# A two-layer attention and retention trunk on one core: value products a round later, the first span outputs in column parts, later sines, evenly pulled side work, rows turned and outputs stored in one

## The chip, the cores and the metric

The kernel runs on one core of a Trainium2 chip. A core has a matrix engine (TensorE; PE in the profile, PEld for its weight loads), a vector engine (DVE), a scalar engine (ACT), GpSimd (POOL), and SyncE (SP), which issues the DMA transfers here. The metric is the time of one execution on the device in microseconds (us). The kernel before takes 2097.04 us, the median of three runs (2094.75 to 2097.13).

## What is computed

Two layers over a sequence of 2048 tokens of width 1024 (float32), then a last RMS norm. In each layer half of the mixing width goes through chunked softmax attention (8 heads of 64; a token sees its chunk of 64 and the 8 chunks before, with a relative bias), the other half through retention (4 heads of 128, rotary phases, decays per head):

```python
def hybrid_layer(x, norm_gain, w_in, w_out, rel_bias, cos, sin):
    hn = rms_norm(x, norm_gain)
    aq, ak, av, ag, rq, rk, rv, rg = jnp.split(hn @ w_in, cuts, axis=-1)
    ya = chunked_rel_attention(aq, ak, av, rel_bias)
    yr = chunkwise_retention(rq, rk, rv, cos, sin)
    y = jnp.concatenate([ya * jax.nn.silu(ag), yr * jax.nn.silu(rg)], axis=-1)
    return x + y @ w_out
```

## The kernel before

**Precision.** Products run in float16 with three terms: every operand is split into a high half and a low remainder, and high times high, high times low and low times high are summed.

**Tiles.** Tokens go in 16 tiles of 128, four of which make a span (n = 0 to 3, 512 columns). The heads go in four groups s: two attention heads and one retention head each. For each layer l, group s and span n there are two stages. `dense_T` (L608) makes four outputs with the tokens in columns, j = 0 to 3: queries, keys, retention queries, retention keys; each is 24 matmuls of 512 columns (three terms, eight slices of the width) in three rounds of eight, into one of two accumulators (psD). `dense_V` (L738) makes values and gates for the span's four token tiles, a = 0 to 3, again 24 matmuls in three rounds each. After it, ACT and DVE empty the accumulator (L760 to L770); the tanh of the gates (L761) lies in a buffer `gt` (five of them), which later holds the gate.

**Rounds.** `run()` (L1152) sets the order of everything. In each round it emits eight dense matmuls, then what `later(k, fn)` (L595) had deferred to this round, then one step of the attention of the span before, then some steps of side work, taken by `pull` from generators that were handed to `push` (L1128). It pulls the whole number above (open steps)/(rounds left).

**Attention.** `attention` (L778) takes eight units (four tiles, two heads), three rounds each: in the first `qk`, in the second a part of the decayed retention product, in the third the retention product. `qk` (L785) makes the scores S on PE (L800, L801; one PSUM buffer); DVE adds the bias and takes the maximum (L804), turns it into the exponent's offset (L806); ACT takes the exponential (L807) and copies it to a high half (L809), POOL subtracts for the low half (L810), and a round later SP transposes both halves by DMA (L812) into `pT` (two buffers). The scores lie in buffers of tag `sc`, the halves in `pq`, two of each. The value product `pv` (L815 to L822) of a unit runs six rounds after its scores, at the start of the round of the unit after next, ahead of that unit's scores. A round later `out_` divides by the sum of weights, multiplies by the gate (L826 to L832), and for the second head stores both heads' columns to y in DRAM (L835).

**Retention.** `decayed` (L870) makes the product of keys and queries and writes it masked to the next 128 columns of its PSUM tile; `retention` (L884) adds the carried state, and `fin` (L923) applies norm and gate and stores to y.

**Normalized rows.** `norms_from_input` (L1166), `residual` (L987) and, for y, the output stage make rows of 1024 in a high and a low half: `rows_hi` (L225, ACT), `rows_lo` (L229, DVE), then `transpose_rows` (L235): two DMA transposes on SP (L236, L237) into `hTh` and `hTl`. The rows lie in the attention's `sc` and `pq` buffers (`row_pair`, L221).

**Rotary tables.** `tables` (L83) works out cosines and sines of one span in small steps of side work; the two sines are L121 and L122, and eight stores follow (L129 to L132). `dense_T` loads the tables of a span in two DMAs (L616, L617).

**Output stage.** `wout` (L1066) multiplies y's tiles with the output weights, six rounds per tile (L1105), while the last span's attention still runs. Per tile it loads y, squares it on ACT into its row buffer (`y_squares`, L955), scales, makes the halves and turns them (`y_turn`, L966); `wout_first` (L1053) does this for the first two tiles as side work, in ten steps.

**Order on the queues.** The order on PE, ACT, DVE and POOL is the order of emission, by hand. The order on SP follows a planner's cost model, except at the start, where it is written out. An instruction that waits holds up all behind it on its engine.

Of the kernel before, what the change touches and what calls it, by code (L numbers as in the profile page):

```python
# [18 lines left out]
P = 128  # L19
# [8 lines left out]
def hybrid_trunk(ctx: ExitStack, tc: tile.TileContext, x, pos, gain, gcol, w_in, w_out, rel, fgain,  # L28
# [33 lines left out]
    pool.memset(mhalf, -0.5)  # L62
    invf_sb = cp.tile([P, 1], F32, tag="invf", name="invf_sb")
# [6 lines left out]
    tab_d = [dp.tile([2, P, 512], F32, tag=f"tab{n}", name=f"tab{n}") for n in range(NS)]  # L70
# [12 lines left out]
    def tables(n, wk):  # L83

        ang, k, r, k2 = wk
# [34 lines left out]
        yield  # L120
        act.activation(r, ang, AF.Sin)  # L121
# [4 lines left out]
        for hf in range(2):  # L126
            sl = slice(hf * 64, hf * 64 + 64)
            cs = slice(hf * 256, hf * 256 + 256)
            sp.dma_start(tab_d[n][0, 0:64, cs], k2[sl, :])  # L129
            sp.dma_start(tab_d[n][0, 64:128, cs], k2[sl, :])  # L130
            sp.dma_start(tab_d[n][1, 0:64, cs], ang[sl, :])
            sp.dma_start(tab_d[n][1, 64:128, cs], r[sl, :])  # L132
# [3 lines left out]
    TAB_STEPS = 19  # L136
# [78 lines left out]
    def hT_of(l, n):  # L215
        if (l, n) not in hT:
            hT[l, n] = (hp.tile([P, KT, 512], F16, tag="hTh", name=f"hTh{l}_{n}"),
                        hp.tile([P, KT, 512], F16, tag="hTl", name=f"hTl{l}_{n}"))
        return hT[l, n]

    def row_pair(nm):  # L221
        return (b2.tile([P, 1280], F16, tag="sc", name=f"rh{nm}")[:, 0:D],
                b2.tile([P, 1280], F16, tag="pq", name=f"rl{nm}")[:, 0:D])
# [11 lines left out]
    def transpose_rows(rows, dh, dl):  # L235
        sp.dma_start_transpose(out=dh, in_=rows[0])  # L236
        sp.dma_start_transpose(out=dl, in_=rows[1])  # L237

    class Tok:


        def __init__(self, t, xt, rows):
            self.t, self.x, self.rows, self.nm = t, xt, rows, f"n0_{t}"
            self.hh, self.hl = (h_[:, :, t % 4 * P:(t % 4 + 1) * P] for h_ in hT_of(0, t // 4))
# [21 lines left out]
        def hi(self):  # L266
            if self.rows:
                self.rw = (self.rows[:, 0:D], self.rows[:, D:2 * D])
                act.activation(self.rw[0], self.x, AF.Copy)
                return  # L270
# [3 lines left out]
        def lo(self):  # L274
            if self.rows:
                dve.tensor_tensor(self.rw[1], self.x, self.rw[0], op=ALU.subtract)
                return
# [4 lines left out]
        def dma(self):  # L282
            transpose_rows(self.rw, self.hh, self.hl)
# [324 lines left out]
    def dense_T(l, s, n, g, st):  # L608
        hh, hl = hT[l, n]
        nm = f"{l}_{s}_{n}"  # L610
        st.tabc = b1.tile([P, 512], F32, tag="tabc", name=f"tabc{nm}")
        st.tabs = b1.tile([P, 512], F32, tag="tabs", name=f"tabs{nm}")
# [14 lines left out]
        def evacuate(j, ps):  # L627
            if j == 0:
                st.q = b2.tile([P, 2, 2, 512], F16, tag="q", name=f"q{nm}")
                qq = b1.tile([P, 2, 512], F16, tag="qq", name=f"qq{nm}")  # L630
# [10 lines left out]
            elif j == 1:  # L641
                st.k = b3.tile([P, 2, 512], F16, tag="k", name=f"k{nm}")
                kk = b1.tile([P, 2, 512], F16, tag="swp", name=f"kk{nm}")
                kh, kl = kk[:, 0, :], kk[:, 1, :]
                act.activation(kh, ps, AF.Copy, scale=2.0 ** -16)

                def k_rest():
                    dve.scalar_tensor_tensor(out=kl, in0=ps, scalar=2.0 ** -16, in1=kh, op0=ALU.mult, op1=ALU.subtract)
                    sp.dma_start(st.k[0:64, 0, :], kh[0:64, :])
                    sp.dma_start(st.k[64:128, 1, :], kh[64:128, :])  # L650
                    sp.dma_start(st.k[64:128, 0, :], kl[0:64, :])
                    sp.dma_start(st.k[0:64, 1, :], kl[64:128, :])

                soon(k_rest)
            else:
                w = 5 - j
                rot = b2.tile([P, w, 512], F16, tag=f"rot{j}", name=f"rot{nm}_{j}")
                if j == 2:
                    raw = rot[:, 1:3].rearrange("p a c -> p (a c)").bitcast(F32)
                else:  # L660
                    raw = b1.tile([P, 512], F32, tag="qq", name=f"raw{nm}")
                act.activation(raw, ps, AF.Copy, scale=2.0 ** -16)

                def swap(rot=rot, raw=raw, j=j):
                    swp = b1.tile([P, 512], F32, tag="swp", name=f"swp{nm}_{j}")
# [20 lines left out]
                    later(d, turned(raw, raw, st.tabc, ALU.mult))  # L686
                    later(d + 1, turned(swp, swp, st.tabs, ALU.mult))
# [30 lines left out]
        for j in range(2 if first else 0, 4):  # L718
# [19 lines left out]
    def dense_V(l, s, n, g, st):  # L738
        hh, hl = hT[l, n]
# [38 lines left out]
    def attention(l, s, n, g, st, prev, nxt):  # L778
# [4 lines left out]
        ya = {}  # L783

        def qk(a, hx):  # L785
# [10 lines left out]
            for j0, j1 in zip(cuts, cuts[1:]):  # L796
# [5 lines left out]
            v = b2.tile([P, 640], F32, tag="sc", name=f"sc{u.nm}")[:, 0:w]  # L802
            m = b2.tile([P, 1], F32, tag="mq", name=f"mq{u.nm}")
            dve.tensor_tensor_reduce(out=v, in0=S[:, 0:w], in1=g.bias[hx][:, 640 - w:640], scale=1.0, scalar=-3.0e38,  # L804
                                     op0=ALU.add, op1=ALU.max, accum_out=m)
            dve.tensor_scalar(m, m, g.nc[:, 0:1], LN_PSC, op0=ALU.mult, op1=ALU.add)  # L806
            act.activation(v, v, AF.Exp, bias=m[:, 0:1], scale=g.c[:, 0:1])  # L807
            pq = b2.tile([P, 1280], F16, tag="pq", name=f"pq{u.nm}")
# [6 lines left out]
        def pv(u):  # L815
            t = 4 * n + u.a
            o = psR.tile([P, 512], F32, tag="small", name=f"o{u.nm}")
            for b, (q_, a_) in enumerate(u.kts):
# [3 lines left out]
                pe.matmul(o[:, 0:65], u.p[:, u.nb + b, :], v_[:, 0:65], start=False, stop=(b == u.nb - 1))  # L822

# [692 lines left out]
```

## Time and profile before

| | |
|---|---|
| median of 3 runs | 2097.04 us (2094.75 to 2097.13) |
| profiled execution | 2094.75 us |
| its span (first to last instruction) | 2092.8 us |
| granted TensorE clock, mean | 0.991 |
| PE busy | 2004.4 us, 96% |
| DVE / ACT / POOL busy | 64% / 55% / 21% |
| SP's issues | 1084 us in all |

A view of waits names the waiting engine and line, the tile it waited for with the engine and line that made it, then the total in us, the number of waits and the longest. A view of windows gives for each stretch its length, the busy time and count of PE, PEld, DVE, ACT and POOL, the granted clock, the busy share of the DMA engines and GB/s. A timeline row gives the start and the length in us, engine, line, operation, output and inputs; in brackets stands the idle time before it and what ended it. Matmul ends are modelled, so a start-to-start distance says more than a matmul's length. A row of the chain of waits has start, length and what was running. A row of groups has line, engine, operation, shapes and count, then busy us, mean ns of one, idle us before and what ended it.

### The profile page before, as it was taken

Reading aid. Unit: us, or ns where it says so; the run is one execution under the profiler, and the core shown is the slowest. Engines: PE = TensorE matmul, PEld = TensorE weight load, DVE = VectorE, ACT = ScalarE, POOL = GpSimd, SP = SyncE. Lnnn points to the kernel's source line nnn. Section 1 sums busy time; section 2 is a strip of 40 time slices with the busy share of each in tenths; the row PEclk is TensorE's granted clock in tenths of the full one; section 3 lists DMA queues with packets and bytes.
Section 4 is the critical chain, followed back from the end, with each engine's and each line's share of the span. In section 5 each row is a group of like instructions: output and inputs, shape, how many; then the busy total and the mean of one; then the engine's idle time right before and its main releaser. Section 6 shows DMA issues by size and latency. Waiting matters only on the chain.

```text
span 2092.8 us, 39599 instructions
## 1 busy us (share of the span) xinstructions
PE 2004.4 (96%) x14014; PEld 1049.4 (50%) x14014; DVE 1343.8 (64%) x4031; ACT 1141.3 (55%) x2522; POOL 432.9 (21%) x509
## 2 busy tenths in 40 slices
PE   6888999999999999998999999999999999998998
PEld 4344455555555555444444555555555555554443
DVE  7676666666656666576654666666666667656643
ACT  7455665556565654455444546554655565455432
POOL 1022222222122212121000222222222222222100
PEclk9999999999999999999999999999999999999999
DMA  8767674557476764599965556655655776558874
GB/s 247 171 127 162 136 166 114 115 112 159 110 169 133 161 166 99 113 211 260 219 185 113 120 102 142 130 121 106 155 123 118 178 156 162 117 100 183 212 199 123
DMA packets 645702, 313.65 MB, mean 150 GB/s; under 512 B 459232, under 2 KB 602080, under 8 KB 645504
## 3 DMA queue, kind: packets, MB, share of 16 engines
q1 hardware_dynamic: 645504, 311.12, 66.4%
q8 instruction: 110, 1.80, 0.4%
q14 instruction: 88, 0.72, 0.1%
HBM read 123.26 MB, written 41.98 MB: 79 GB/s over the span
## 4 chain that ended last, share of the span: by engine, by line
PE 55%; DMA 7%; DVE 5%; ACT 3%; issue 1%; SPq 1%; POOL 0%; POOLq 0%; DVEq 0%; ACTq 0%
PE dT L731 18%; PE dV L752 15%; PE dO L1105 12%; DMA pT<-pq 2%; PE r L860 2%; PE S L801 2%; PE S L800 2%; PE o L820 1%; PE o L821 1%; PE o L822 1%; DVE sc L804 1%; DMA swp<-rot 1%; DMA yhy<-rhy 1%; ACT sc L807 1%; ACT pq L809 1%
## 5 line engine op out<-in xcount | busy, mean ns | idle before, releaser
L810 POOL TENSOR_TENSOR pq<-sc,pq 128x640 f16<-128x640 f32 (+4 forms) x256 | 323.8, 1265 | 1175.9 <-issue 590.7
L807 ACT ACTIVATE sc<-sc,mq,cT 128x640 f32<-128x640 f32 (+4 forms) x256 | 218.5, 853 | 558.1 <-DVE mq L806 413.7
L752 PE MATMUL dV<-whV,hTh 128*128 128x512 f16 x1024 | 354.5, 382 | 13.0 <-DVE gt L770 12.8
L731 PE MATMUL dT<-hTh,whT 128*128 128x512 f16 x1008 | 349.4, 382 | 14.7 <-DMA hTh<-hTl 9.6
L752 PE MATMUL dV<-wlV,hTh 128*128 128x512 f16 x1024 | 354.1, 381 | 0.0
L752 PE MATMUL dV<-whV,hTl 128*128 128x512 f16 x1024 | 354.0, 381 | 0.0
L731 PE MATMUL dT<-hTl,whT 128*128 128x512 f16 x1008 | 346.6, 379 | 0.0
L731 PE MATMUL dT<-hTh,wlT 128*128 128x512 f16 x1008 | 346.6, 379 | 0.0
L752 PEld LDWEIGHTS <-hTh 128*128 128x128 f16 x2048 | 197.3, 98 | 227.7 <-DVE gt L770 16.4
L731 PEld LDWEIGHTS <-whT 128*128 128x128 f16 x2016 | 192.9, 98 | 221.6 <-issue 24.1
L804 DVE CUSTOM_DVE_ANT_0 sc<-S,bias 128x640 f32<-128x640 f32 (+4 forms) x256 | 188.4, 736 | 78.8 <-PE S L801 61.1
L1105 PE MATMUL dO<-whO,yly 128*128 128x512 f16 x512 | 194.1, 379 | 2.4 <-DMA yly<-rly 2.4
L1105 PE MATMUL dO<-whO,yhy 128*128 128x512 f16 x512 | 194.0, 379 | 1.2 <-DVE gt L770 0.6
L1105 PE MATMUL dO<-wlO,yhy 128*128 128x512 f16 x512 | 194.0, 379 | 0.0
L809 ACT ACTIVATE pq<-sc 128x640 f16<-128x640 f32 (+4 forms) x256 | 171.5, 670 | 10.9 <-DMA pT<-pq 3.0
L1105 PEld LDWEIGHTS <-yhy 128*128 128x128 f16 x1024 | 99.6, 98 | 115.1 <-issue 0.8
L752 PEld LDWEIGHTS <-hTl 128*128 128x128 f16 x1024 | 99.7, 98 | 105.0 <-issue 2.8
L800 PE MATMUL S<-k,q 128*128 128x128 f16 (+3 forms) x592 | 143.1, 268 | 7.9 <-DVE mq L804 7.9
L731 PEld LDWEIGHTS <-wlT 128*128 128x128 f16 x1008 | 97.2, 98 | 101.8 <-issue 1.1
L820 PE MATMUL o<-v,pT 128*128 128x65 f16 x1120 | 129.6, 193 | 10.2 <-DMA pT<-pq 9.7
L801 PE MATMUL S<-k,q 128*128 128x128 f16 (+3 forms) x592 | 130.5, 268 | 0.0
L820 PEld LDWEIGHTS <-pT 128*128 128x128 f16 x1120 | 105.3, 97 | 49.2 <-DMA pT<-pq 21.3
(350 smaller groups left out, 3352.7 us busy)
## 6 DMA issues: line engine op xcount, KB each, us to landing
q<-qq SPq DMA_DIRECT2D x128, 128.0 KB, 2.7
yyy<-y_d SPq DMA_DIRECT2D x32, 512.0 KB, 4.6
stT<-in_w_in_dram SPq DMA_DIRECT2D x27, 512.0 KB, 4.8
stV<-in_w_in_dram SPq DMA_DIRECT2D x26, 512.0 KB, 4.5
k<-kk SPq DMA_DIRECT2D x128, 64.0 KB, 2.0
swp<-rot SPq DMA_DIRECT2D x64, 128.0 KB, 2.5
tabc<-tab SPq DMA_DIRECT2D x32, 256.0 KB, 2.7
tabs<-tab SPq DMA_DIRECT2D x32, 256.0 KB, 2.9
```

What stands on the lines that cost most here:

```text
L731: pe.matmul(ps, w_[:, j, kt, :], h_[:, kt, :], start=(m == 0), stop=(m == 23))
L752: pe.matmul(ps, h_[:, kt, a * P:(a + 1) * P], w_[:, kt, :], start=(m == 0), stop=(m == 23))
L800: pe.matmul(o, st.q[:, hx, 0, cs], k_, start=True, stop=False)
L801: pe.matmul(o, st.q[:, hx, 1, cs], k_, start=False, stop=True)
L804: dve.tensor_tensor_reduce(out=v, in0=S[:, 0:w], in1=g.bias[hx][:, 640 - w:640], scale=1.0, scalar=-3.0e38, op0=ALU.add, op1=ALU.max, accu ...
L807: act.activation(v, v, AF.Exp, bias=m[:, 0:1], scale=g.c[:, 0:1])
L809: act.activation(pq[:, 0:w], v, AF.Copy)
L810: pool.tensor_tensor(pq[:, w:2 * w], v, pq[:, 0:w], op=ALU.subtract)
L820: pe.matmul(o[:, 0:65], u.p[:, b, :], v_[:, 0:65], start=(b == 0), stop=False)
L821: pe.matmul(o[:, 0:64], u.p[:, b, :], v_[:, 65:129], start=False, stop=False)
L860: pe.matmul(out_, w_, m_, start=(i == 0), stop=(i + 1 == len(pairs)))
L1105: pe.matmul(ps, h_[:, kt, :], w_[:, kt, :], start=(m == 0), stop=(m == 23))
```

## The change

- *Scores:* high and low rows, and scores with their halves, share one buffer of tag `spq` (two of 5 KB per partition) in place of `sc` and `pq`. The sign and scale of the exponent go into L804 as a per-partition scale with a minimum instead of a maximum; the offset is then one addition, on POOL instead of DVE.
- *Rows:* `hTh` and `hTl` are halves of one tile, so that one transpose turns both; the last y tile keeps two.
- *Value products:* `pv` follows the round's yield, seven rounds after the scores. Both heads of a tile share one PSUM tile; a single `out_` divides both, in place in the gate buffer, and one store per tile goes out when both attention and retention have finished.
- *Column parts:* for l = s = 0 and n > 0 the first two outputs are made in parts of 128 columns, the last token's part last, 32 short matmuls a round.
- *Tables:* the sines one step later for n > 0, four stores instead of eight, one load instead of two.
- *Side work:* `run` carries a fraction over, so that the steps are spread evenly. `wout_first` has two empty steps ahead of the first `y_turn`.
- *Also:* the decayed product is masked in place; query halves, key halves and the rotary scratch share one buffer tag `qk`, the table tile is `tab`, and `y_turn` writes to these.

```diff
-        ang, k, r, k2 = wk
+        ang, r, k2, k = (wk[:, i * 256:(i + 1) * 256] for i in range(4))
...
         yield
+        if n:
+            yield
         act.activation(r, ang, AF.Sin)
         act.activation(k2, k, AF.Sin)
...
-        for hf in range(2):
-            sl = slice(hf * 64, hf * 64 + 64)
-            cs = slice(hf * 256, hf * 256 + 256)
-            sp.dma_start(tab_d[n][0, 0:64, cs], k2[sl, :])
-            sp.dma_start(tab_d[n][0, 64:128, cs], k2[sl, :])
-            sp.dma_start(tab_d[n][1, 0:64, cs], ang[sl, :])
-            sp.dma_start(tab_d[n][1, 64:128, cs], r[sl, :])
+        parts = wk[:, 0:768].rearrange("p (a c) -> p a c", c=256)
+        for h in range(2):
+            for hf in range(2):
+                sp.dma_start(tab_d[n][h * 64:h * 64 + 64, :, hf * 256:hf * 256 + 256],
+                             parts[hf * 64:hf * 64 + 64, h:3:2 - h])
...
     def row_pair(nm):
-        return (b2.tile([P, 1280], F16, tag="sc", name=f"rh{nm}")[:, 0:D],
-                b2.tile([P, 1280], F16, tag="pq", name=f"rl{nm}")[:, 0:D])
+        return halves_of(b2.tile([P, 2560], F16, tag="spq", name=f"rw{nm}")[:, 0:2 * D])
...
-    def transpose_rows(rows, dh, dl):
-        sp.dma_start_transpose(out=dh, in_=rows[0])
-        sp.dma_start_transpose(out=dl, in_=rows[1])
+    def transpose_rows(rows, dst):
+        sp.dma_start_transpose(out=dst, in_=rows[2])
...
-            sp.dma_start(st.tabc, tab_d[n][0])
-            sp.dma_start(st.tabs, tab_d[n][1])
+            sp.dma_start(st.tab, tab_d[n])
...
+        parts = (l, s) == (0, 0) and n > 0
+        if parts:
+            ps, m = [None] * 2, 0
+            for (j, a) in ((0, 0), (0, 1), (0, 2), (1, 0), (1, 1), (1, 2), (0, 3), (1, 3)):
+                if a == 0:
+                    ps[j] = psD.tile([P, 512], F32, tag="dense", name=f"dT{nm}_{j}")
+                cs = slice(a * P, (a + 1) * P)
+                for i in range(24):
+                    w_, h_ = ((g.h, hh), (g.l, hh), (g.h, hl))[i // KT]
+                    pe.matmul(ps[j][:, cs], w_[:, j, i % KT, :], h_[:, i % KT, cs], start=(i == 0), stop=(i == 23))
+                    m += 1
+                    if m % 32 == 0 and m < 192:
+                        yield
+                if a == 3:
+                    evacuate(j, ps[j])
+            yield
-        for j in range(2 if first else 0, 4):
+        for j in range(2 if first or parts else 0, 4):
...
+        def finished(a):
+            left[a] -= 1
+            if left[a] == 0:
+                t = 4 * n + a
+                sp.dma_start(y_d[t].rearrange("p (a s c) -> p a s c", a=2, c=P)[:, :, s],
+                             st.g[a].rearrange("p (a c) -> p a c", a=2))
...
-            v = b2.tile([P, 640], F32, tag="sc", name=f"sc{u.nm}")[:, 0:w]
+            spq = b2.tile([P, 2560], F16, tag="spq", name=f"spq{u.nm}")
+            v, pq = spq[:, 0:1280].bitcast(F32)[:, 0:w], spq[:, 1280:2560]
             m = b2.tile([P, 1], F32, tag="mq", name=f"mq{u.nm}")
-            dve.tensor_tensor_reduce(out=v, in0=S[:, 0:w], in1=g.bias[hx][:, 640 - w:640], scale=1.0, scalar=-3.0e38,
-                                     op0=ALU.add, op1=ALU.max, accum_out=m)
-            dve.tensor_scalar(m, m, g.nc[:, 0:1], LN_PSC, op0=ALU.mult, op1=ALU.add)
-            act.activation(v, v, AF.Exp, bias=m[:, 0:1], scale=g.c[:, 0:1])
-            pq = b2.tile([P, 1280], F16, tag="pq", name=f"pq{u.nm}")
+            dve.tensor_tensor_reduce(out=v, in0=S[:, 0:w], in1=g.bias[hx][:, 640 - w:640], scale=g.nc[:, 0:1],
+                                     scalar=3.0e38, op0=ALU.add, op1=ALU.min, accum_out=m)
+            pool.tensor_tensor(m, m, lnp, op=ALU.add)
+            act.activation(v, v, AF.Exp, bias=m[:, 0:1], scale=-1.0)
...
             def out_():
-                rl = b2.tile([P, 1], F32, tag="rl", name=f"rl{u.nm}")
-                dve.reciprocal(rl, o[:, 64:65])
-                dve.tensor_tensor(rl, rl, g.ka, op=ALU.mult)
...
-                if u.hx == 1:
-                    sp.dma_start(y_d[t][:, s * P:(s + 1) * P], y)
+                rl = b2.tile([P, 2], F32, tag="rl", name=f"rl{u.nm}")
+                dve.reciprocal(rl, o2[:, 0:2, 64])
+                dve.tensor_scalar(rl, rl, g.ka[:, 0:1], None, op0=ALU.mult)
+                for hx in range(2):
+                    y = st.g[u.a][:, hx * 64:hx * 64 + 64]
+                    dve.scalar_tensor_tensor(out=y, in0=o2[:, hx, 0:64], scalar=rl[:, hx:hx + 1], in1=y, op0=ALU.mult,
+                                             op1=ALU.mult)
+                finished(u.a)
...
-            flow(1)
-            u = qk(a, hx)
-            yield
+            u = qk(a, hx)
+            yield
+            flow(1)
...
-        later(1, lambda: dve.tensor_tensor(r1[:, P:2 * P], r1[:, 0:P], g.msk, op=ALU.mult))
+        later(1, lambda: dve.tensor_tensor(r1, r1, g.msk, op=ALU.mult))
...
-            u.h = b1.tile([P, KT, P], F16, tag=("tabc", "qq")[u.t % 2], name=f"yh{u.nm}")
-            u.lo = b1.tile([P, KT, P], F16, tag=("tabs", "swp")[u.t % 2], name=f"yl{u.nm}")
-        transpose_rows(u.rows, u.h, u.lo)
+            yT = b1.tile([P, 2 * KT, P], F16, tag=("tab", "qk")[u.t % 2], name=f"yT{u.nm}")
+            u.h, u.lo = yT[:, 0:KT], yT[:, KT:2 * KT]
+            transpose_rows(u.rows, yT)
...
-                    (lambda: rows_lo(u.rows, u.y, u.sy), lambda: y_squares(v)), (lambda: y_turn(u), lambda: y_scale(v, go)),
+                    (lambda: rows_lo(u.rows, u.y, u.sy), lambda: y_squares(v)), (), (), (lambda: y_turn(u), lambda: y_scale(v, go)),
...
-        left = thirds
+        left, debt = thirds, 0.5
...
-                pull(min(-(-todo // max(left, 1)), todo))
+                debt += todo / max(left, 1)
+                pull(min(int(debt + 0.01), todo))
+                debt -= int(debt + 0.01)
...
-                    push(wout_first(l, go, us), 10)
+                    push(wout_first(l, go, us), 12)
```

More of the change, by code (lines that the diff above doesn't have):

```diff
@@ L69, in hybrid_trunk @@
     x_d = [dp.tile([P, D], F32, tag=f"x_d{t}", name=f"x_d{t}") for t in range(NT)]
-    tab_d = [dp.tile([2, P, 512], F32, tag=f"tab{n}", name=f"tab{n}") for n in range(NS)]
+    tab_d = [dp.tile([P, 2, 512], F32, tag=f"tab{n}", name=f"tab{n}") for n in range(NS)]
     TWO_PI = 6.283185307179586
@@ L274, in lo @@
         def lo(self):
-            if self.rows:
+            if self.rows is not None:
                 dve.tensor_tensor(self.rw[1], self.x, self.rw[0], op=ALU.subtract)
@@ L685, in swap @@
                     d = 5 if j == 2 and first else 3
-                    later(d, turned(raw, raw, st.tabc, ALU.mult))
-                    later(d + 1, turned(swp, swp, st.tabs, ALU.mult))
+                    later(d, turned(raw, raw, st.tab[:, 1], ALU.mult))
+                    later(d + 1, turned(swp, swp, st.tab[:, 0], ALU.mult))
                     later(d + 2, turned(raw, raw, swp, ALU.add))
@@ L1192, in dma @@
         def dma(k):
[L1193 removed]
+            transpose_rows(us[k].rows, us[k].h[2])
         us = []
@@ L1273, in hybrid_trunk @@
     sp.dma_start(invf_sb, invf)
-    t0 = tables(0, [gp.tile([P, 256], F32, tag="gt", name=f"wk{i}") for i in range(4)])
+    t0 = tables(0, b2.tile([P, 2560], F16, tag="spq", name="wk").bitcast(F32)[:, 0:1024])
     go_on(t0)
```

111 lines of the change are left out of this document (58 added, 53 removed).

## The prediction, made before the changed kernel was run

> **What bounds the kernel.** Read first: the page's busy shares, then the waits of PE in total, then busy time by stage.
>
> ```profile
> span 2092.8 us, 39599 instructions
> PE 2004.4 (96%) x14014; PEld 1049.4 (50%) x14014; DVE 1343.8 (64%) x4031; ACT 1141.3 (55%) x2522; POOL 432.9 (21%) x509
> ```
> ```profile
> PE dV L752 <- DVE gt L770: 12.8, 6, 4.9
> PE o L820 <- DMA pT<-pq: 9.7, 11, 2.2
> PE dT L731 <- DMA hTh<-hTl: 9.6, 1, 9.6
> PE S L800 <- DVE mq L804: 7.9, 4, 3.3
> ...
> PE dT L731 <- DMA hTh<-rhn: 2.8, 1, 2.8
> ...
> PE dT L731 <- issue: 2.2, 1, 2.2
> ```
> ```profile
> 50.00:100.00 50.00, 40.16 (x199) 18.42 (x197) 32.59 (x81) 24.55 (x50) 4.32 (x11) 0.90 0.72 164
> ...
> 400.00:450.00 50.00, 50.00 (x395) 27.45 (x394) 31.83 (x88) 23.99 (x58) 13.93 (x13) 1.00 0.47 98
> ...
> ```
> TensorE's program is written out by hand and it is the bound: 2092.8 - 2004.4 = 88.4 us idle in all. The second number of a window is PE's busy time: at 400 us PE has no gap, at 50 us it stands for 9.8 us and the granted clock (third from the end) falls to 0.90. Most edits (fewer stores, both heads divided at once, the mask in place, the minimum that scales) work on DVE, ACT and SP, which have room in the full stretches, so I cost them at nothing there: PE covers them. What can be won is the six rows of waits, and the slow clock that some leave behind. The change must be costed stage by stage.
>
> **A. Start of span n=1** (joint transposes, four table stores for eight, one table load for two, column parts).
>
> ```profile
> 53.64 0.59 SPq L132 DMA_DIRECT2D tab<-wk  x1
> ...
> 63.79 1.25 SPq L236 DMA_TRANSPOSE hTh<-hTh  x1
> ...
> 71.86 0.50 SPq L666 DMA_DIRECT2D swp<-raw  x1
> ...
> 74.73 2.92 SPq L237 DMA_TRANSPOSE hTl<-hTl  x1
> ```
> ```profile
> 78.11 0.69 DVE L670 TENSOR_TENSOR raw<-raw,tabc 128x512 f32<-128x512 f32 x1 [7.20 <-DMA swp<-raw]
> ```
> ```profile
> 78.91 3.26 PE L731 MATMUL dT<-hTh,whT 128*128 128x512 f16 x8 [9.64 <-DMA hTh<-hTl]
> ```
> SP issues without a gap here. PE waits 9.64 us for the last token's transpose, issued at 74.73, and DVE 7.20 us for a swap of key halves issued at 71.86 behind it all. Four stores less take 4 x 0.64 (the spacing of such stores, of which this row is the last) = 2.56 us off SP; a joint transpose costs one issue for two, saving some 1.2 us each: three of them stand ahead of 71.86, so that the swap goes out 2.6 + 3.6 = 6.2 us earlier. The columns need only their own token, so PE starts on token 4 and meets the last one after 192 short matmuls. Then the rotated keys are late next, by what is left of DVE's wait, 7.20 - 6.2 = 1. Bounds: 0 (the DMA engines themselves are the limit: share 0.72) and 9.64 + 1.37 of slow clock = 11.0. I take **+7.5**, nearer to the upper as SP, not the data, sets the order.
>
> **B. Sines later.**
>
> ```profile
> 124.36 1.28 ACT L121 ACT_TABLE_LOAD   x1
> ...
> 126.54 1.28 ACT L761 ACT_TABLE_LOAD   x1
> ```
> ```profile
> 129.54 0.61 PE L752 MATMUL dV<-whV,hTh 128*128 128x512 f16 x1 [4.88 <-DVE gt L770]
> 129.94 0.63 PE L752 MATMUL dV<-whV,hTl 128*128 128x512 f16 x1
> ...
> 192.54 0.61 PE L752 MATMUL dV<-whV,hTh 128*128 128x512 f16 x1 [4.25 <-DVE gt L770]
> ```
> The sines and two table loads stand ahead of a value evacuation, for whose slot PE then waits; its next matmuls come 0.40 us and more apart, twice the full pace (1.73 us for eight, 0.216 each, by the chain's row at 1929.83 in E), for 3.4 and 5.3 us. Both cost 4.88 + 1.7 and 4.25 + 2.6 = 13.4 us. By the counts of steps pulled per round, the sines of n=1 move from round 18's side to just behind the evacuation of round 21, three rounds (6.6 us) ahead of the next; n=2 alike. The table's stores on SP move with them; the next span loads the table some eight rounds into its outputs, so they stay ahead. Bounds 6 (one removed) and 13.4; **+12**.
>
> **C. Starts of n=2 and 3, and the column parts.** Waits of 2.8 and 2.2 (rows above) plus 1.5 of slow clock: +6.5. Against it, 128-column parts:
>
> ```profile
> 31.66 0.61 PE L712 MATMUL dT<-hTh,whT 128*128 128x128 f16 x8
> ...
> 37.01 0.38 PE L731 MATMUL dT<-hTh,whT 128*128 128x512 f16 x1
> ```
> ```profile
> L731 PEld LDWEIGHTS <-whT 128*128 128x128 f16 x2016 | 192.9, 98 | 221.6 <-issue 24.1
> ...
> L631 ACT ACTIVATE qq<-dT 128x512 f16<-128x512 f32 x32 | 18.8, 586 | 7.6 <-PE dT L731 6.6 <-PE dT L712 0.3
> ```
> The twelve groups from 31.66 to 37.01 are 96 matmuls in 5.35 us, 55.7 ns each. Three spans x 192 x 55.7 ns = 32.1 us replace 3 x 48 x 0.216 = 31.1: -1.0. The third output reuses the first's accumulator right away, while ACT (586 ns) and DVE (about as much) still read it, with 1.3 us of parts to cover it: -1 a span, 0 to -3 (bounds). Sum 6.5 - 1.0 - 3 = **+2.5** (-5 to +5.4). The Trainium skill, page "TensorE: Matmul & The Clock Gate", section "Back-to-back issue gap", speaks against this edit: in a sustained stream of weight loads and matmuls it gives about 81 ns for a matmul of 128 columns. By it the parts would cost 576 x 0.081 - 31.1 = 15.6 us (an estimate), not 1.0. The row of 55.7 ns is such a stream, and I go by it.
>
> **D. Value products a round later.**
>
> ```profile
> 953.88 0.20 PE L820 MATMUL o<-v,pT 128*128 128x65 f16 x1 [2.19 <-DMA pT<-pq]
> ```
> The longest of the 11 waits for transposed scores is 2.19; a round is eight dense matmuls, 1.73 us, 2.2 with the rest, so all go. Of the 9.7 us, 6.2 lie in the output stages (four about 900 to 954, one at 1909); the rest is **+3.5** (0 to 3.5). The division, a round later too, has nobody on PE close behind it. The two buffers of transposed scores stay taken a round longer: a product now comes one round (2.2 us) behind the scores of the unit after next, whose transpose is issued 4.8 us behind those scores (1950.95 to 1955.75 in the next part), so no transpose waits.
>
> **E. Scores and halves in one buffer of two.** Before, scores were free once POOL had subtracted, and the halves had two buffers of their own. Now DVE's L804 of a later unit waits until the transpose has landed. In the full stretches two slots cover it, at two units of 6.5 us. In the output stages a row of y holds one slot for the whole period:
>
> ```profile
> 1929.46 1.04 ACT L958 ACTIVATE rhy<-yyy 128x1024 f16<-128x1024 f32 x1
> ...
> 1942.35 1.04 ACT L958 ACTIVATE rhy<-yyy 128x1024 f16<-128x1024 f32 x1
> ```
> ```profile
> 1913.77 0.82 DVE L804 CUSTOM_DVE_ANT_0 sc<-S,bias 128x640 f32<-128x640 f32 x1
> ...
> 1944.12 0.82 DVE L804 CUSTOM_DVE_ANT_0 sc<-S,bias 128x640 f32<-128x640 f32 x1
> ...
> 1950.95 0.81 DVE L804 CUSTOM_DVE_ANT_0 sc<-S,bias 128x640 f32<-128x640 f32 x1
> ```
> ```profile
> 1955.75 1.94 SPq L812 DMA_TRANSPOSE pT<-pq  x1
> ```
> ```profile
> 1929.83 1.73 PE dO L1105 x8
> ...
> 1949.24 4.14 DMA pT<-pq
> ```
> ```profile
> 933.50 5.12 DMA pT<-pq
> ```
> Seven units from 1913.77 to 1950.95 come 6.2 us apart, with the eighth 6.3 (the value I use). A joint slot would be held from 1944.12 to 1949.24 + 4.14 = 1953.38, 9.26 us; from 1950.95 to 1955.75 + some 3.5, 8.3. If the other slot is a row's, units come every h us, and after PE's slack (6.3 less the scores' own matmuls, 1.2, and L804, 0.82: 4.3 us) a layer loses 7(h - 6.3) - 4.3. The joint transposes shorten SP's queue a little: h = 8.2 gives 9 us a layer, 18 for two, less the 6.2 of D: **-12**. Bounds: +6.2 (h of 6.9 or less, or both slots free in turn) and -33 (9.26 in both layers, and D's 6.2 not won). Behind a waiting L804 stand the output evacuations, which have 6 us to spare, and the next tile's low half.
>
> The new POOL addition lies in the same chain:
>
> ```profile
> L806 DVE TENSOR_SCALAR mq<-mq,ncT 128x1 f32<-128x1 f32 x256 | 54.8, 214 | 9.1
> ...
> L921 POOL TENSOR_TENSOR rss<-rss,mhalf 128x1 f32<-128x1 f32 x128 | 72.5, 567 | 139.1 <-DVE rss L920 130.6 <-ACT rv L762 7.2 <-DVE m2T L325 1.3
> ```
> 214 ns before; POOL's nearest row, a power, bounds it by 567, below by some 190. It is nearest to a plain addition, 300; all of it is in h, and elsewhere it is covered by two buffers: a slot is wanted again 13 us (two units) later and held for some 8.5.
>
> **F. First y tile two empty steps later.**
>
> ```profile
> 877.29 0.82 DVE L804 CUSTOM_DVE_ANT_0 sc<-S,bias 128x640 f32<-128x640 f32 x1 [5.11 <-DMA yhy<-rhy]
> ```
> ```profile
> 878.17 0.27 PE L800 MATMUL S<-k,q 128*128 128x128 f16 x1 [3.28 <-DVE mq L804]
> ...
> 1891.00 0.27 PE L800 MATMUL S<-k,q 128*128 128x128 f16 x1 [3.18 <-DVE mq L804]
> ```
> Two rows of y hold both slots when a unit's scores want one. With steps spread evenly the second row's squares fall behind those scores in the same round, so the scores get through: 3.28 + 3.18 and 4.7 of slow clock behind them, 11 us, can go. But now these squares wait on ACT for a slot, some 5 us, with evacuations queued behind, and the first turn is a round later. Bounds +11 and -6; **+5**.
>
> **Sum:** 7.5 + 12 + 2.5 + 3.5 - 12 + 5 = 18.5; span 2092.8 - 18.5 = 2074.3. The profiled execution took 2094.75, 1.95 over its span: 2076.3; the median of the runs is 2.3 above it. Between the two: **2077**.
>
> **Rivals.**
> - More: rows and scores find slots in turn (E at 0) and F comes whole (+11): 18.5 + 12 + 6 = 36.5, time 2060. For it: rows free their slot for a moment each period. Against: from 1929.46 to 1942.35 one row follows the other.
> - Less at the starts: DMA engines set A (+2) and the handover costs its bound (C at -4): 12 less, 2089. For it: DMA share 0.72 there; against: SP's gapless queue.
> - Column parts bound by weight loads: at 98 ns (row of L731's loads) they cost 56.4 - 31.1 = 25.3, 24 more than forecast: 2101, no change. Against it stands 55.7 ns. By the Trainium skill's 81 ns (page and section named in C), 14.6 more: 2091.
> - Slower, the shared buffer: at h = 10.5 E is -(2 x (7 x 4.2 - 4.3) - 6.2) = -44, the sum -13.5, time 2109. It outweighs the rest from h = 9.5 on. For it: the 5.12 us landing at 933.50, and 9.26 in one row; against: 8.3 in the next, and fewer transposes on SP.
> - The change doesn't do what it says: the later sines and products only hand their waits to the next evacuation; B, D and F give nothing, 2095 to 2098.
>
> **Numbers.** A run tells no change within 0.2%, 4 us. Forecast 0.46 (own range 2064 to 2088), more 0.18, less at the starts 0.13, weight loads 0.05, slower 0.12, nothing 0.06. Faster: 0.46 + 0.18 + 0.13 + half of nothing = 0.80; same 0.03 + 0.05 = 0.08; slower 0.12. The range reaches halfway into the "more" case and to the edge of slower: 2052 to 2100.
>
> **What would show it.** A: the wait at the start of n=1 below 4 us and SP's swap out by 67. B: no table load ahead of a value evacuation, the row of gt waits below 3 us. C: short matmuls at 56 ns. D: no wait for transposed scores. E: L804 waiting for the landing of the previous transpose in the output stages, units 8 us apart; 6.3 would prove the term wrong, 10 makes it slower. F: no wait of S at 878. Wrong altogether if new idle time shows up in the full stretches, where I costed everything at nothing.

## The result and the profile after

The changed kernel is slower.

| | before | changed |
|---|---|---|
| median | 2097.09 us (4 runs) | 2239.68 us (4 runs) |
| ratio | | 1.0679, 95% interval 1.066 to 1.0697 |
| span of the profiled run | 2092.8 us | 2237.8 us |
| granted clock, mean | 0.991 | 0.972 |

From the page of the changed kernel, the span and the busy times:

```profile
span 2237.8 us, 39810 instructions
PE 2043.6 (91%) x14446; PEld 1083.1 (48%) x14446; DVE 1266.0 (57%) x3519; ACT 1118.3 (50%) x2522; POOL 521.9 (23%) x766
```

DVE and ACT work less than before and the kernel takes 145 us more: 106 us of it is idle time of PE (194 against 88), the other 39 PE's longer busy time, as the lower clock would have it: 2004.4 x 0.991 / 0.972 = 2043.6. PE's waits in the changed kernel, in total, times and longest:

```profile
PE dT L753 <- DVE gt L792: 24.2, 14, 2.7
PE r L890 <- DVE sh L898: 22.2, 9, 3.8
PE dT L733 <- DVE gt L792: 22.2, 5, 8.5
PE dV L774 <- DVE gt L792: 18.6, 8, 5.3
PE S L829 <- DVE mq L834: 17.2, 13, 3.1
...
PE o L851 <- DMA pT<-spq: 3.0, 2, 2.0
```

The waits for transposed scores fell from 9.7 to 3.0 and the one for the rows of n=1 is gone. In their place PE waits for the gate `gt` at three lines, 65 us in all, where it waited 12.8. The gate comes from DVE (L792), which follows ACT's tanh (L783). ACT's waits show why; the second line did not exist before:

```profile
ACT spq L837 <- POOL mq L836: 573.4, 250, 6.5
ACT gt L783 <- DMA y_d<-gt: 144.1, 30, 9.1
```

ACT stands still for 144 us, in 30 waits over the 32 spans, all of them at a span's fourth tile, until a store of y out of a gate buffer has landed. One of these places, from the timeline (start, length, engine, line, operation; in brackets the idle time and its releaser):

```profile
611.11 0.48 DVE L863 SCALAR_TENSOR_TENSOR gt<-o,rl,gt 128x64 f32<-128x64 f32 x2
...
612.92 0.26 ACT L782 ACTIVATE v<-dV 128x128 f16<-128x128 f32 x1
613.09 1.23 SPq L841 DMA_TRANSPOSE pT<-spq  x1
614.43 0.56 SPq L811 DMA_DIRECT2D y_d<-gt  x1
...
616.79 0.47 ACT L783 ACTIVATE gt<-dV,ughV 128x256 f32<-128x256 f32 x1 [3.61 <-DMA y_d<-gt]
...
617.55 0.29 DVE L788 SCALAR_TENSOR_TENSOR v<-dV,v 128x128 f16<-128x128 f32 x1 [5.76 <-ACT rv L784]
...
618.49 0.39 PE L753 MATMUL dT<-hT,whT 128*128 128x512 f16 x1 [2.23 <-DVE gt L792]
```

DVE writes y into the gate buffer until 611.6, SP issues the store at 614.43 behind a transpose, and it has landed at 616.8. ACT wanted the buffer at 613.2. DVE then waits 5.76 us for ACT, everything queued on either engine slips, and PE stands for 2.23 us until DVE has made the gate. The next such place, a span later, ends in the same way:

```profile
676.71 0.47 ACT L783 ACTIVATE gt<-dV,ughV 128x256 f32<-128x256 f32 x1 [3.21 <-DMA y_d<-gt]
```
```profile
678.41 0.39 PE L753 MATMUL dT<-hT,whT 128*128 128x512 f16 x1 [1.60 <-DVE gt L792]
```

Where the time goes along the program shows best at marks that all kernels share: the exponentials, 256 in number. This table, worked out from the timelines, has the start of a unit's exponential before (in us from the span's start), and how much later (or earlier, -) it starts in other kernels. The experiments below tell of them: e1_gate6 is the changed kernel with six gate buffers, f2_split has separate score buffers too, h1_split_dveadd also the addition on DVE, and r5_evenfirst is the version that beats both.

```
layer, group, span, unit   before   changed  e1_gate6  f2_split  h1_split_dveadd  r5_evenfirst
0, 0, 0, 0                   83.4      -5.2      -3.2      -3.5             -5.6          -2.7
0, 0, 1, 0                  144.1       8.6       6.4       2.3              0.0           3.0
0, 1, 0, 0                  321.9      30.1      15.5       7.2              4.3           1.0
0, 3, 0, 0                  736.4      55.8      20.8      11.8              7.8          -2.9
0, 3, 3, 0                  902.0      60.6      20.7       8.3              1.2          -7.8
1, 0, 0, 0                 1131.1      77.3      35.6      12.6              3.4          -4.7
1, 3, 0, 0                 1749.3     125.1      42.8      20.0             10.2          -7.8
1, 3, 3, 0                 1914.9     130.3      43.1      16.8              4.2         -13.5
1, 3, 3, 7                 1958.6     146.6      58.8      18.1              3.3         -14.9
```

The start of n=1 gains its 5 us. Then the changed kernel loses everywhere: 35 us by the end of the first group, some 80 in the rest of the two layers, and 16 in each output stage.

### The profile page after: what moved, and what is told of

Same layout as the page of the kernel before. It is cut to its first block, busy times and chain, and to the rows that moved or that the text cites. A ratio compares the mean times of both kernels' runs of the same rounds, so it can differ in the third digit from the quotient of the medians.

```text
span 2237.8 us, 39810 instructions
## 1 busy us (share of the span) xinstructions
PE 2043.6 (91%) x14446; PEld 1083.1 (48%) x14446; DVE 1266.0 (57%) x3519; ACT 1118.3 (50%) x2522; POOL 521.9 (23%) x766
## 5 line engine op out<-in xcount | busy, mean ns | idle before, releaser
L774 PE MATMUL dV<-whV,hT 128*128 128x512 f16 x2048 | 603.5, 385 | 20.4 <-DVE gt L792 18.6
L753 PE MATMUL dT<-hT,whT 128*128 128x512 f16 x1920 | 557.6, 382 | 29.6 <-DVE gt L792 24.2
L837 ACT ACTIVATE spq<-spq,mq 128x640 f32<-128x640 f32 (+4 forms) x256 | 194.9, 762 | 575.3 <-POOL mq L836 573.4
L774 PEld LDWEIGHTS <-hT 128*128 128x128 f16 x3072 | 289.7, 99 | 330.3 <-DVE gt L792 21.9
L839 POOL TENSOR_TENSOR spq<-spq 128x640 f16<-128x640 f32 (+4 forms) x256 | 320.7, 1253 | 415.2 <-issue 347.1
L774 PE MATMUL dV<-wlV,hT 128*128 128x512 f16 x1024 | 353.2, 381 | 0.0
L753 PE MATMUL dT<-hT,wlT 128*128 128x512 f16 x960 | 334.3, 382 | 0.0
L1136 PE MATMUL dO<-whO,yTy 128*128 128x512 f16 x960 | 296.4, 387 | 23.2 <-ACT whO L336 16.3
L834 DVE CUSTOM_DVE_ANT_0 spq<-S,bias,ncT 128x640 f32<-128x640 f32 (+4 forms) x256 | 202.9, 793 | 46.7 <-DMA pT<-spq 26.8
L1136 PE MATMUL dO<-wlO,yTy 128*128 128x512 f16 x480 | 185.5, 387 | 1.5 <-DVE wlO L339 1.5
L783 ACT ACTIVATE gt<-dV,ughV 128x256 f32<-128x256 f32 x128 | 59.6, 466 | 144.1 <-DMA y_d<-gt 144.1
```

What stands on the lines that cost most here:

```text
L753: pe.matmul(ps, w_[:, j, kt, :], h_[:, kt, :], start=(m == 0), stop=(m == 23))
L774: pe.matmul(ps, h_[:, kt, a * P:(a + 1) * P], w_[:, kt, :], start=(m == 0), stop=(m == 23))
L837: act.activation(v, v, AF.Exp, bias=m[:, 0:1], scale=-1.0)
L839: pool.tensor_tensor(pq[:, w:2 * w], v, pq[:, 0:w], op=ALU.subtract)
L1136: pe.matmul(ps, h_[:, kt, :], w_[:, kt, :], start=(m == 0), stop=(m == 23))
```

## The experiments

Beside every run stands the kernel before on the same chip, with medians from 2093.1 to 2095.2 us; the ratios are to it. Line numbers shift a little from kernel to kernel.

**The gate buffer.** The changed kernel with a sixth one:

```diff
-            gt = gp.tile([P, 256], F32, tag="gt", name=f"gt{nm}_{a}")
+            gt = gp.tile([P, 256], F32, tag="gt", name=f"gt{nm}_{a}", bufs=6)
```

> The changed kernel with six gate buffers instead of five. Theory G (the gate buffer, which now also carries y until its store has landed, is not free when the fourth tile's tanh wants it, and ACT stands still in front of it, 144 us in all): that wait vanishes, PE's waits for the gate fall from 65 us to under 10, the time from 2240 to 2110, give or take 25. Rival S (scores and halves sharing one buffer, and the addition on POOL, set the loss): the wait on ACT vanishes too, but the time stays above 2200.

2151.87 us, ratio 1.0281 (1.0251 to 1.0311). ACT's wait is gone, and 88 us with it: theory G for the larger part, but 40 us short of its number, and PE's waits for the gate fall to 35 us, not under 10. The next three runs are on the same cause. With the value products early again and five buffers:

```diff
-            u = qk(a, hx)
-            yield
-            flow(1)
+            flow(1)
+            u = qk(a, hx)
+            yield
```

> The changed kernel with the value products back ahead of the scores, a round earlier. Theory G: the third tile's y store goes out a round (2.2 us) sooner, so ACT's wait falls from 4.8 us a span to some 2.6 and the time to about 2165. Theory V (the later products cost nothing; the store alone is the matter): the wait stays near 4.8 us and the time above 2215.

2172.72 us, 1.038 (1.035 to 1.0411). ACT's wait for the store falls from 144.1 to 31.2 us. A round earlier is nearly early enough.

> Six gate buffers and the value products early. Theory G: within 15 us of six buffers alone, with PE's waits for transposed scores back at some 10 us. If the later products harm in another way than through the gate buffer: more than 20 us below six buffers alone.

2154.65 us, 1.0294 (1.0264 to 1.0324): the same as six buffers alone, with 23.5 us of waits for transposed scores where some 10 were expected. From the other side, the kernel before with this part alone: `fin` and `out_` write y into the gate buffer and call `finished`.

```diff
-                y = ya[u.a]
...
+                y = st.g[u.a][:, u.hx * 64:u.hx * 64 + 64]
...
-                if u.hx == 1:
-                    sp.dma_start(y_d[t][:, s * P:(s + 1) * P], y)
+                if u.hx == 1:
+                    finished(u.a)
```

> The kernel before, with only this part of the change: attention and retention write y into the gate buffer and one store per tile goes out when both are done; five buffers, products early. Theory G: slower, 2130 to 2165, with ACT's tanh waiting for the store some 2 to 3 us a span. Rival (PE's three rounds of slack hide such a wait, as the prediction had it): 2090 to 2105.

2123.85 us, 1.0147 (1.0107 to 1.0187), a little under the expected range, with 36.6 us of ACT's waits for the store. So the in-place y costs 30 us without the later products, and the later products add to it. The same with six buffers:

> The kernel before with y in the gate buffer and one store per tile, and six gate buffers. With five it took 2124. Theory G (only the missing sixth buffer costs): 2090 to 2097. Rival (the joint store is later or longer for its readers, or the chain on DVE): above 2105.

2098.0 us, 1.0013 (1.0003 to 1.0022), 1 us above the expected range. Theory G: writing in place and storing once cost next to nothing where a buffer is free.

**The joint score buffer.** In the kernel with six gate buffers, DVE's minima in layer 1's output stage:

```profile
1964.74 0.88 DVE L834 CUSTOM_DVE_ANT_0 spq<-S,bias,ncT 128x640 f32<-128x640 f32 x1 [2.23 <-DMA pT<-spq]
...
1972.68 0.88 DVE L834 CUSTOM_DVE_ANT_0 spq<-S,bias,ncT 128x640 f32<-128x640 f32 x1 [2.27 <-DMA pT<-spq]
...
2015.20 0.88 DVE L834 CUSTOM_DVE_ANT_0 spq<-S,bias,ncT 128x640 f32<-128x640 f32 x1 [2.24 <-DMA pT<-spq]
```

Seven units in a row wait for a transpose of the unit before, 50.46 / 6 = 8.4 us apart. Next, separate buffers again, of the same size in all; the rows are turned in two, and the scratch of the first rotary tables moves to the buffers of tag `q`:

```diff
-            spq = b2.tile([P, 2560], F16, tag="spq", name=f"spq{u.nm}")
-            v, pq = spq[:, 0:1280].bitcast(F32)[:, 0:w], spq[:, 1280:2560]
+            v = b2.tile([P, 640], F32, tag="sc", name=f"sc{u.nm}")[:, 0:w]
+            pq = b2.tile([P, 1280], F16, tag="pq", name=f"pq{u.nm}")
```

> Six gate buffers, and scores, halves and rows back in separate buffers of the same size (two of each), the rows turned in two transposes. Theory E (the joint buffer serializes the units at 8.4 us in the output stages, 15 us a layer): each output stage falls back to units about 6.3 us apart, the time by 25 to 35 us to 2117 to 2127. Rival (something else holds the units, such as the addition on POOL or the later products): units stay at 8 us, time above 2140.

2112.73 us, 1.0084 (1.0046 to 1.0122), 39 us less, more than expected. The units of layer 1's output stage are 6.3 us apart again (1930.47 to 1974.52 for eight). In the table, layer 0's output stage (from 0, 3, 3, 0 to 1, 0, 0, 0) costs 14.9 with the joint buffer and 4.3 without, layer 1's 15.7 and 1.3: 25 us of the 39. Most of the rest lies in the first group, where rows of the next span's tokens use the same buffers: 15.5 against 7.2. The buffers and the transposes in two are not tested apart.

**The addition on POOL.**

```diff
-            pool.tensor_tensor(m, m, lnp, op=ALU.add)
+            dve.tensor_scalar(m, m, LN_PSC, None, op0=ALU.add)
```

> Six gate buffers and the offset's addition on DVE instead of POOL. Theory (it is hidden, but for a share in the hold of the joint buffer): within 6 us of 2152. Rival (POOL's queue delays the exponential; ACT waits 597 us for it in all, as it waited for DVE before): more than 15 us faster.

2138.01 us, 1.0206 (1.0161 to 1.025; two runs, 6 us apart): 14 us faster, close to the rival's bound.

> The three causes taken away together: six gate buffers, separate buffers for scores, halves and rows, the offset's addition on DVE. Separate buffers alone gave 2113 and the addition 14 us with the joint buffer. If the addition costs by the length of the chain that holds the joint buffer: it is worth 7 us at most here, 2106 to 2113. If it costs by itself (POOL's queue ahead of the exponential): the whole 14, 2095 to 2102.

2095.68 us, 1.0012 (1.0 to 1.0024). The addition is worth 17 us here, though no joint buffer makes the chain's length count: the first reading falls. With these three causes away the loss is gone: 88 + 39 + 17 = 144 us.

**Column parts and their order.** Without the parts, six gate buffers:

> Six gate buffers and no column parts: the first two outputs of layer 0, group 0 in 512 columns again. Six buffers alone take 2152; against the kernel before, their loss up to the end of the first group is 16 us, and PE waits 14 us for the gate ahead of the parts and 7.6 for the evacuation ahead of the third output. Theory P (the parts need both accumulators at once, and hand one over while it is read): 10 to 20 us faster, 2132 to 2142. Rival (the parts win their wait for the last transpose as forecast, the loss comes from elsewhere in that stage): slower by 5 or more, above 2157.

2155.87 us, 1.0291 (1.0258 to 1.0324): not faster, so theory P falls; 4 us slower, with intervals that overlap, and short of the rival's bound too. PE's waits for rows at the three starts are back:

```profile
PE dT L753 <- DMA hT<-rwn: 27.8, 2, 14.2
...
PE dT L753 <- DMA hT<-hT: 8.2, 1, 8.2
```

With the parts these 36 us are gone, but waits for the gate and for the handover fill most of their place. Another order of the parts, on the kernel with the three causes away:

```diff
-            for (j, a) in ((0, 0), (0, 1), (0, 2), (1, 0), (1, 1), (1, 2), (0, 3), (1, 3)):
+            for (j, a) in ((0, 0), (0, 1), (0, 2), (1, 0), (1, 1), (0, 3), (1, 2), (1, 3)):
```

> The kernel with all three causes away (2096), with the column parts in another order: the first output's last part ahead of the second output's third, so that twice as much PE work stands between the first output's end and its accumulator's reuse. If the handover's wait (8.1 us in three) is real time lost: 2089 to 2093. If the first part's waits for the gate, or the last token's rows, take its place: 2094 to 2100.

2094.46 us, 0.9996 (0.9986 to 1.0006). The handover's wait (8.1 us in the kernel it is compared with) falls to 1.5 us, the time is 1 us less: other waits filled its place.

**Value products later.** On the kernel before, alone:

> The kernel before with the value products a round later and nothing else. As forecast in step D: all 9.7 us of waits for transposed scores go, time 2084 to 2090 beside some 2094 for the kernel before on this chip. Rival (the later products hold buffers that somebody waits for, and hand the wait on): not faster, 2093 or more.

2100.13 us, 1.0029 (1.0017 to 1.004): slightly slower. PE's waits in this kernel:

```profile
PE S L800 <- DVE mq L804: 13.5, 9, 5.6
...
PE r L860 <- DVE ya L832: 4.9, 5, 2.8
...
PE o L820 <- DMA pT<-pq: 3.2, 3, 2.1
```

The waits for transposed scores fall by 6.5 us, those of the next scores rise by 5.6, and those of the retention products (L860) for the division (L832) are new. Undone in the kernel without the three causes, they turn out to pay there:

> As the kernel with all three causes away, and the value products early again. The later products alone cost the kernel before 0.3%. If that holds here too: some 6 us faster than with the later products. If the later products pay where the rest of the change stands: slower by 5 or more.

2114.73 us, 1.0106 (1.0089 to 1.0123): 19 us slower, with 22.2 us of waits for transposed scores. What the step is worth depends on the rest.

**Later sines and even pulling.** On the kernel before:

> The kernel before with the later sines and the evenly pulled side work alone. As forecast in step B: PE's two waits of 4.9 and 4.3 us for the gate behind the sines go, 2081 to 2088 beside 2094. Rival (the wait is handed on to another evacuation, or the rows of the next span come later): 2091 to 2100.

2124.99 us, 1.0159 (1.014 to 1.0178), far outside both expectations. PE's waits for the gate fell to 4.2 us as forecast, but at the starts of n=2 and n=3 its timeline has

```profile
148.22 3.57 PE L733 MATMUL dT<-hTh,whT 128*128 128x512 f16 x8 [14.32 <-DMA hTh<-rhn]
...
222.07 3.57 PE L733 MATMUL dT<-hTh,whT 128*128 128x512 f16 x8 [14.84 <-issue]
```

where it waited 2.2 and 2.8 before. Steps pulled evenly come later than steps pulled in whole numbers rounded up, and the last rows with them. The sines alone, pulled as before:

> The kernel before with the sines one step later for n > 0 and the side work pulled as before. The later sines and the even pulling together cost 32 us, with PE waiting 14.3 and 14.8 us for rows at the starts of n=2 and n=3. If the even pulling alone makes the rows late: those waits are back at 2.8 and 2.2 and, with the waits behind the sines gone, the time is 2081 to 2090 beside 2093. If the later sines harm: above 2096.

2096.7 us, 1.0004 (0.9995 to 1.0014). Neither reading holds: the time is above 2096, but the kernel before took 2095.24 beside it, and the starts of n=2 and n=3 now wait 4.8 and 4.9 us, and the gate 9.2. What the later sines win behind them they lose at the next start. The large waits come from the pulling.

**The empty steps ahead of the first y tile.**

> As the one before, and the first y tile's turn two empty steps later. As forecast in step F: another 5 us (0 to 11) faster, the wait of 3.3 us of the scores at the output stage's start gone. Rival (the square of the second row now waits on ACT for a buffer, and evacuations behind it): 0 to 8 us slower than without.

2120.44 us, 1.0139 (1.0122 to 1.0156): 4.5 us faster than without them.

> As the one before, and the two empty steps ahead of the first y tile's turn taken out. As forecast in step F the empty steps gain 5 (0 to 11): then this one is slower by that. Beside the kernel before with even side work they gained 4.5. If they gain only where the scores' buffers are tight: the same within 3.

2097.01 us, 1.0007 (0.9995 to 1.0018): 2.5 us slower without them. The sign is the forecast's both times; intervals of this width settle neither.

**A version that beats both.** The kernel with the three causes away and the other order of parts falls some 6 us behind in layer 1. The even pulling is now left to the first group and the last span of each layer's last group:

```diff
-                debt += todo / max(left, 1)
-                pull(min(int(debt + 0.01), todo))
-                debt -= int(debt + 0.01)
+                if ring.get("even", True):
+                    debt += todo / max(left, 1)
+                    pull(min(int(debt + 0.01), todo))
+                    debt -= int(debt + 0.01)
+                else:
+                    pull(min(-(-todo // max(left, 1)), todo))
...
+                ring["even"] = (l, s) == (0, 0) or n == NS - 1 and s == NSW - 1
```

> As the kernel with the three causes away and the other order of parts (2094.5), with the even pulling only in the first group and in the last span of each layer's last group, the old pulling elsewhere. In that kernel the attention units of layer 1 drift 7 us behind those of the kernel before between its first group and its last. If the even pulling makes that drift: it goes, and the time is 2086 to 2091, below both kernels. If something else in the change makes it: 2093 to 2097, and none of these parts beats the kernel before.

2078.53 us, 0.9924 (0.991 to 0.9937): faster than both kernels, and below the expected range, so more than the drift was won. PE's waits there:

```profile
PE dT L738 <- DVE gt L797: 12.2, 5, 5.0
PE dV L779 <- DVE gt L797: 7.4, 7, 3.9
...
PE S L834 <- DVE mq L839: 3.5, 7, 1.6
...
PE o L856 <- DMA pT<-pq: 2.4, 1, 2.4
```

Waits for transposed scores and for the scores' buffer are down from 9.7 and 7.9. In the table the lead grows by 4.9 us from the first to the last span of layer 0's last group and by 5.7 in layer 1's; the first y tiles are prepared there. Last, the addition on POOL once more, in this kernel:

> The kernel that beats both (2078.5), with the offset's addition on POOL again. From the start of the scores' minimum to the exponential it takes 1.32 us on POOL and 1.08 on DVE, the mean over the units. If this only costs where the even pulling leaves waits standing: within 5 us of 2078.5. If the addition on POOL costs by itself, as it did with the even pulling (17 us with separate buffers): 2090 to 2098.

2096.74 us, 1.0012 (0.9998 to 1.0025): 18 us lost by moving one addition. The whole gain hangs on it.

## Why the prediction was wrong, point by point

**The step that failed** stands in its first part: "Most edits (fewer stores, both heads divided at once, ...) work on DVE, ACT and SP, which have room in the full stretches, so I cost them at nothing there: PE covers them." Storing y out of the gate buffer was costed as a saving of stores. But the part also lengthens the time for which a gate buffer is taken: from DVE's last read to the landing of a store, some 5 us later in the rows at 611 to 617, and the later products add a round. With five buffers the fourth tile's tanh then finds none free. The shares of busy time don't show this; a count of who holds which buffer until when would have. I made that count for the scores' buffers (E) and the transposed scores' (D), and not for this one. It measured 88 us, where nothing stood in the sum. As the prediction's last sign of being wrong had it, new idle time showed up in the full stretches. The rival "slower" named the wrong buffer.

**E, the joint buffer:** the mechanism was right, the size was not. The units came 8.4 us apart (forecast 8.2), but the two stages lost 14.9 and 15.7 us, not 9, and 10.6 and 14.4 of that went with the joint buffer. 7 x (8.4 - 6.3) = 14.7 would be the loss without PE's slack of 4.3 us; how much of that slack there was, no run shows by itself. The first group's share wasn't in the sum. Separate buffers won 39 us, for a cost put at 18 (12 after the 6.2 us of D).

**The addition** was said to be "covered by two buffers" outside the output stages, and its length was put between 190 and 567 ns. Most came out at the lower bound, but not all:

```profile
184.73 1.22 DVE L235 TENSOR_TENSOR rwn<-xin,rwn 128x1024 f16<-128x1024 f32 x1
...
184.89 1.10 POOL L836 TENSOR_TENSOR mq<-mq,lnp 128x1 f32<-128x1 f32 x1 [5.25 <-DVE mq L834]
...
1700.10 0.19 POOL L836 TENSOR_TENSOR mq<-mq,lnp 128x1 f32<-128x1 f32 x1 [7.63 <-DVE mq L834]
```

In the changed kernel 177 of the 256 took 0.19 us; the other 79 took 0.24 to 1.17 us, 28 of them over 1 us, and the mean of all is 354 ns. Each of the 79 ran beside a DVE operation of 256 to 1024 columns and ended 47 to 54 ns after it, which none of the 177 did (worked out from the timelines). In 78 of them that operation had begun first, as at 184.73.

From the start of the minimum to the exponential a unit took 1.33 us with it and 1.09 with the addition on DVE (means over the 256 units of the last two kernels, worked out from their timelines). That is some 63 us over all units, 44 of them by the long additions. It cost 14, 17 and 18 us of the time in three settings. The extra waits of PE are spread over the gate, the scores, the carried state and the y tiles; which of the long additions cost that time stays open.

**A** was right in place, for a reason that was half wrong. PE's wait of 9.64 us for the rows of n=1 became one of 2.02 us for the gate, and the first unit came 5 us earlier (forecast 7.5). But the swap went out at 68.17, 3.7 us earlier and not 6.2, so A's sign (out by 67) failed:

```profile
53.94 3.49 SPq L240 DMA_TRANSPOSE hT<-hT  x1
...
60.74 6.12 SPq L240 DMA_TRANSPOSE hT<-hT  x2
...
68.17 0.50 SPq L672 DMA_DIRECT2D tmp<-tmp  x1
...
69.42 3.75 SPq L240 DMA_TRANSPOSE hT<-hT  x1
```

A joint transpose held SP for 3.1 to 3.8 us here, two single ones in the same stretch before for 2.6 to 4.6: the 1.2 us that each was to save are not there.

**B:** the wait behind the sines went, but only moved to the next start, as the last rival had it; its other half, the even pulling, makes rows late. The column parts take these waits away, but no run shows that the time comes back with them. **C:** the short matmuls ran as forecast, and neither parts nor handover moved the time measurably. The pace in the changed kernel:

```profile
140.19 0.61 PE L733 MATMUL dT<-hT,wlT 128*128 128x128 f16 x8
...
141.53 0.61 PE L733 MATMUL dT<-hT,wlT 128*128 128x128 f16 x8
```

24 matmuls in 1.34 us are 55.8 ns each, between other matmuls and weight loads. The 81 ns of the Trainium skill's page "TensorE: Matmul & The Clock Gate", section "Back-to-back issue gap", don't appear here.

**D:** alone it only hands its waits on to the next scores; with the rest in place it is worth 19 us. **F:** 2.5 and 4.5 us for a forecast of 5, but not by the waits named. PE's waits of 3.28 and 3.18 us for the scores at the output stages' starts were gone with the even pulling alone; the longest left there was 1.14 us.

The terms other than E, 30.5 us by forecast (36.7 with the 6.2 us of D that E was to take back), came to 15 us (2093.77 - 2078.53) in the version that beats both. That version has single transposes and even pulling in a few places only, so it is no exact test of the sum.

## What to carry to other kernels

Before writing a result into a buffer that another step refills, count the buffer's holders round by round up to the landing of the store, and compare with the number of buffers; a store or two saved is nothing beside an engine that waits in front of its queue. In a kernel whose bound engine is full, "the other engines have room" covers work, not waits: each added wait must be followed to what is queued behind it. Some parts of a change pay only together with others (the later products lost 7 us alone and won 19 with the rest), so testing each alone on the kernel before can show a loss for a part that wins.

## What the runs showed of the hardware

An addition of one column on POOL in place of one on DVE of 0.15 us cost 14 to 18 us of some 2100, although POOL is busy a quarter of the time. It took 0.19 us in 177 of 256 cases, and up to 1.17 us in the 79 in which a DVE operation ran beside it to within 47 to 54 ns of its end. DVE's minimum with a scale per partition took 793 ns on average against 736 for the maximum without:

```profile
L834 DVE CUSTOM_DVE_ANT_0 spq<-S,bias,ncT 128x640 f32<-128x640 f32 (+4 forms) x256 | 202.9, 793 | 46.7 <-DMA pT<-spq 26.8 <-PE S L830 7.2 <-PE dO L1136 4.8
L836 POOL TENSOR_TENSOR mq<-mq,lnp 128x1 f32<-128x1 f32 x256 | 90.7, 354 | 828.3 <-DVE mq L834 711.9 <-DVE m2V L331 33.4 <-DVE rl L859 28.4
```

ACT's exponential with a constant scale took 762 ns, against 853 with one per partition.
